# Listing the picked experts by products of one-hots, with prefix products at later ticks and six dense blocks

## The chip, the cores and the metric

The kernel runs on one core of one Trainium2 chip, in one launch. The metric is the device time of an execution in microseconds; less is better. The engines are TensorE (PE, with its weight loads as PEld), VectorE (DVE), ScalarE (ACT), GpSimd (POOL) and SyncE (SP), which only issues transfers here.

## The reference

Two transformer blocks are computed in float32, on 256 tokens of width 2048. The change touches only the last part of the second block, a mixture of 16384 small experts, of which each token picks 16 in each of 8 heads:

```python
def block(xt):
    q = (xt @ wq).reshape(-1, PEER_HEADS, 2, PEER_HALF)
    s = jnp.einsum('thpc,hpnc->thpn', q, keys)
    sv, si = lax.top_k(s, PEER_TOPK)
    ...
    top_s, top_j = lax.top_k(cand, PEER_TOPK)
    eid = jnp.take_along_axis(cid, top_j, axis=-1)
    gate = jax.nn.softmax(top_s.astype(jnp.float32), axis=-1)
    ue = jnp.take(u, eid, axis=0)
    act = jax.nn.gelu(jnp.einsum('thkd,td->thk', ue, xt).astype(jnp.float32), approximate=False)
    ve = jnp.take(v, eid, axis=0)
    return jnp.einsum('thk,thkd->td', (gate * act).astype(xt.dtype), ve)
```

`u` and `v` have 16384 rows of 2048. The result is added to the block's input and normalised.

## The kernel before

Everything ahead of the experts (both blocks' projections, attention, recurrence, the scores and the top-16) is the same in both kernels. What follows has two stages.

**The u loop.** All 16384 experts are multiplied with all tokens: 128 tiles of 128 experts (`i1`), each 128 x 2048 of `u`, loaded in two halves of 512 KB (L94, issued by SP, three buffers). Each half is split into a high and a low float32r part: `whi` is a cast on ACT (L127), `wlo` a subtraction on DVE (L110). From tile 44 on, 16 pairs of matmuls per tile follow (L281 with 512 columns, L282 with 256), then the addition of two halves (L288, L289) and the evacuation (`evac_u`: gelu on ACT, L1383, and a product with the token weights on DVE, L1384). The result of a tile, 128 experts x 256 tokens, stays in SBUF.

Between the matmuls a generator is advanced by `fill.tick()`: after half and at the end of each half tile, so four times per tile once all tokens are weighed. Each tick runs the generator to its next `yield`; what it issues stands at that place in the engines' queues. From tile 44 on it is `weigh`, which makes the weight of every expert for every token out of one-hots (compares on DVE L1240 and on POOL L1242, products on TensorE L1254 and L1257), four tokens at a time. Then `lists` runs.

**`lists`** counts which experts were picked, by which quarters of the tokens (64 tokens each, a code of four bits), and gives each picked expert a place in a list. There are ten classes of codes with 11 or 7 columns of 128 places each (`CLASSES`), and 22 columns (`CA`) for all experts that find no place in their class. Places come from scans along a partition (L1296, L1316) and two products with a triangular matrix over the partitions (the prefix products, L1302 and L1320). Then the number of each picked expert is written to its place in DRAM (`lst`): one indirect write on POOL for each of the 120 tiles (L1340), 128 elements of 4 bytes each; unpicked experts have an address out of bounds. The list is read back (L1348) and turned into two tables of row numbers (L1351 to L1357): `lv` for rows of `v`, `lact` for rows of `rows`.

Meanwhile `keep` copies the finished tiles 0 to 119 to `rows` in DRAM, four tiles (512 KB) at a time, issued by SP between the loads of `u` (L1367): one or two after each tile, as far as tiles are done.

**The v stage.** The output is a sum over blocks of 128 experts: first the dense ones, the tiles from `NKEY` = 120 on, whose rows of `v` are loaded as they stand (L1478); then the blocks of the list, whose rows of `v` and `rows` are gathered by indirect reads on POOL (L1469), into eight slots. Dense and catch-all blocks are split into high and low parts (L1489, L1490 for `v`, L1493, L1494 for the activations) and take 24 matmuls of 512 columns (L1507). A slot's next gather waits for the split or the products that read it. `rest()` handles list columns beyond `CA`; it is skipped at run time unless more than `CA` x 128 experts need the catch-all places. The output's second half is normalised and written at the end.

Of the kernel before, what the change touches and what calls it, by code (L numbers as in the profile page):

```python
# [9 lines left out]
F32 = mybir.dt.float32  # L10
# [3 lines left out]
U32 = mybir.dt.uint32  # L14
I32 = mybir.dt.int32
AF = mybir.ActivationFunctionType
OP = mybir.AluOpType
# [4 lines left out]
D = 2048  # L22
# [19 lines left out]
N1 = 100  # L42
NKEY, CA = 120, 22
CLASSES = {1: 11, 2: 11, 4: 11, 8: 11, 3: 7, 12: 7, 5: 7, 10: 7, 9: 7, 6: 7}
BASE = {c: NKEY + sum(list(CLASSES.values())[:i]) for i, c in enumerate(CLASSES)}
WL = NKEY + sum(CLASSES.values())
BIG = 2.0 ** 20
HELD, SLOTS, LAST = 2, 8, 4
# [143 lines left out]
def block(ctx, tc, a):  # L192
# [58 lines left out]
    def lane(l):  # L251
        return lnp.tile([128, 512], F32, name=f"lane{l}", bufs=2)
# [953 lines left out]
    lst = dp.tile([128 * WL, 1], F32, name="lst")  # L1206
    lst2 = lst.rearrange("(p w) o -> p (w o)", p=128)
    work = pg.tile([128, 2304], F16, name="work")
    el = work.bitcast(F32)[:, 0:WL]
    pool.memset(el, 0.0)  # L1210
    pool.dma_start(lst2, el)
    pool.dma_start(rows[0:1, 0:WL], el[0:1])
# [65 lines left out]
    def lists(l, cnt):  # L1278
# [20 lines left out]
        dve.tensor_copy(tot, w[:, :, NKEY - 1])  # L1299
        yield  # L1300
        ps = lane(l)
# [15 lines left out]
        dve.tensor_copy(ends[:, 0:1], g[:, NKEY - 1:NKEY])  # L1317
        yield
        ps = lane(l)
# [10 lines left out]
        dve.scalar_tensor_tensor(at, place, -1.0, x, op0=OP.add, op1=OP.add)  # L1330
        yield
        dve.tensor_scalar(to, at, 7, None, op0=OP.logical_shift_right)
        dve.tensor_scalar(at, at, 127, None, op0=OP.bitwise_and)
        dve.tensor_copy(x, at)
        dve.scalar_tensor_tensor(at, x, float(WL), to, op0=OP.mult, op1=OP.add)
        e = work.bitcast(F32)[:, 0:NKEY]
        pool.iota(e, pattern=[[128, NKEY]], base=1, channel_multiplier=1, allow_small_or_imprecise_dtypes=True)
        yield
        for i in range(NKEY):
            d = pool.indirect_dma_start(  # L1340
                out=lst, out_offset=bass.IndirectOffsetOnAxis(ap=at[:, i:i + 1], axis=0), in_=e[:, i:i + 1],
                in_offset=None, bounds_check=128 * WL - 1, oob_is_err=False)
            if i:
                tc.declare_no_dep(d.ins, group="scatter", reason="no two experts have one place")
            tc.add_to_no_dep_group("scatter", d.ins)
            if i % 8 == 7:
                yield
        pool.dma_start(el, lst2)  # L1348
        lact, lv = (pg.tile([128, WL], U32, name=n) for n in ("tab", "tab2"))
        places.extend([lact, lv])  # L1350
        pool.tensor_copy(lact, el)  # L1351
        for q in range(4):

            i = BASE[1 << q]
            x = slice(i, i + CLASSES[1 << q])
            pool.tensor_scalar(lact[:, x], el[:, x], 4.0, float(q), op0=OP.mult, op1=OP.add)
        pool.tensor_scalar(lv, el, 1.0, -1.0, op0=OP.max, op1=OP.add)  # L1357
        yield
# [4 lines left out]
    def keep(i, n):  # L1363

        x, j = act_at(i)
        out = rows[1 + i * 128:1 + (i + n) * 128, :].rearrange("(n p) t -> p n t", p=128)
        nc.sync.dma_start(out, x[:, j:j + n, :])  # L1367

    def act_at(i1):
        for i, j, x in acts:  # L1370
            if i1 < j:
                return x, i1 - i
# [162 lines left out]
    def rest():  # L1535

        raw, x = lt[:, 2 * D:3 * D], lt[:, 3 * D:3 * D + T]
        hi = [sp.tile([128, 1024], F32R, name="whi", bufs=BUFS[1]) for _ in range(4)]
        hi, lo = hi[:2], hi[2:]
# [204 lines left out]
```

## Time and profile before

| | |
|---|---|
| median of 3 runs | 2685.31 us (2666.25 to 2693.32) |
| profiled execution: time, span | 2674.23 us, 2672.4 us |
| mean granted clock of TensorE | 0.979 |
| busy: PE, DVE, ACT, POOL | 2530.4, 1598.2, 1027.4, 816.0 us |
| DMA over the span | 535.39 MB, mean 200 GB/s |

The span runs from the first to the last instruction of the profiled execution. The time of a stage is read from its own stretch, not from the totals: the u loop with `weigh` ends its token products at about 1968 us, `lists` follows, the loop's last matmul starts at 2256.3 us, and the v stage's first at 2260.5 us.

### The profile page before, as it was taken

How to read it: one execution, taken by the hardware profiler on the slowest of the kernel's cores; microseconds unless marked ns; L12 is line 12 of the kernel's file. 1: busy time of each engine (PE TensorE's matmuls, PEld its weight loads, DVE VectorE, ACT ScalarE, POOL GpSimd, SP SyncE). 2: the span in 40 equal slices, each digit the busy share in tenths (PEclk: the TensorE clock that was granted, in tenths of full speed). 3: DMA queues.
4: the chain of work that ended last, by engine and by line, in shares of the span. 5: the costliest groups of instructions: out<-in, count | busy, mean ns of one | idle time of the engine just before them, and what ended most of it. 6: DMA issues, size and time to landing. Idle time of an engine off the chain costs nothing. (4 is left out here: it accounts for less than half of the span.)

```text
span 2672.4 us, 39702 instructions
## 1 busy us (share of the span) xinstructions
PE 2530.4 (95%) x14942; PEld 2049.0 (77%) x14942; DVE 1598.2 (60%) x3174; ACT 1027.4 (38%) x1680; POOL 816.0 (31%) x765
## 2 busy tenths in 40 slices
PE   6899999999998999999999999999988779999996
PEld 1588888888877888888899999888876467655553
DVE  3366566544565766666579898899993245322225
ACT  3233334333445444443544445544442234322221
POOL 2000000000012000000201024988937760567763
PEclk8999999999999999999999999999998889999998
DMA  9733334543464555555555555445456457799995
GB/s 363 296 121 124 125 131 162 183 144 119 142 236 162 170 171 167 187 183 189 204 199 184 172 190 173 159 159 165 159 175 183 149 180 291 284 351 367 357 340 198
DMA packets 148808, 535.39 MB, mean 200 GB/s; under 512 B 20392, under 2 KB 35912, under 8 KB 133504
## 3 DMA queue, kind: packets, MB, share of 16 engines
q1 hardware_dynamic: 116352, 378.99, 42.1%
q0 software_dynamic: 32112, 153.51, 15.6%
q8 instruction: 120, 1.97, 0.3%
q14 instruction: 80, 0.66, 0.1%
q10 hardware_dynamic: 144, 0.26, 0.0%
HBM read 512.60 MB, written 20.09 MB: 199 GB/s over the span
## 5 line engine op out<-in xcount | busy, mean ns | idle before, releaser
L110 DVE TENSOR_TENSOR wlo<-raw,whi 128x1024 fp32r<-128x1024 f32 x577 | 703.6, 1223 | 522.3 <-remote 108.7
L127 ACT CAST whi<-raw 128x1024 fp32r<-128x1024 f32 x577 | 605.4, 1052 | 879.5 <-PE acc L281 163.6
L281 PE MATMUL acc<-ga,whi 128*128 128x512 f32 (+1 forms) x2320 | 848.3, 406 | 24.2 <-issue 22.4
L282 PE MATMUL acc<-ga,wlo 128*128 128x256 f32 (+1 forms) x2320 | 661.3, 285 | 23.7 <-issue 20.9
L281 PEld LDWEIGHTS acc<-ga,whi 128*128 128x128 f32 (+1 forms) x2320 | 444.8, 192 | 129.8 <-issue 27.0
L282 PEld LDWEIGHTS acc<-ga,wlo 128*128 128x128 f32 (+1 forms) x2320 | 446.9, 193 | 44.0 <-issue 37.3
L1242 POOL TENSOR_SCALAR work<-iota,tab 128x128 bf16<-128x128 bf16 x256 | 302.0, 1192 | 88.3 <-PE lane L1257 86.1
L276 PE MATMUL acc<-ga,wlo 128*128 128x256 f32 x704 | 199.4, 283 | 1.3 <-DVE wlo L110 1.3
L274 PE MATMUL acc<-ga,whi 128*128 128x256 f32 x704 | 199.5, 283 | 0.0
L275 PE MATMUL acc<-ga,whi 128*128 128x256 f32 x704 | 199.2, 283 | 0.0
L281 PE MATMUL acc<-X,whi 128*128 128x512 f32 x480 | 173.7, 402 | 0.0
L1490 DVE TENSOR_TENSOR act<-fx,act 128x1024 fp32r<-128x1024 f32 x54 | 64.5, 1223 | 163.7 <-ACT act L1489 156.3
L439 POOL DMA_DIRECT2D gw<-in_w_mod x32 | 17.4, 544 | 465.1 <-DVE gate_b L444 333.5
L1340 POOL DMA_INDIRECT lst<-work,tab x120 | 136.2, 1135 | 57.6 <-issue 36.2
L1507 PE MATMUL acc<-act 128*128 128x512 f32 (+1 forms) x500 | 150.3, 417 | 0.0
L1507 PE MATMUL lane<-act 128*128 128x512 f32 (+1 forms) x476 | 141.6, 412 | 3.8 <-ACT act L1493 3.5
L294 PE MATMUL acc<-whi,X 128*128 128x256 f32 x480 | 136.6, 285 | 0.0
L276 PEld LDWEIGHTS acc<-ga,wlo 128*128 128x128 f32 x704 | 135.1, 192 | 1.7 <-DVE wlo L110 1.7
L1469 POOL DMA_INDIRECT act<-rows,tab x108 | 126.3, 1169 | 32.9 <-issue 30.5
L274 PEld LDWEIGHTS acc<-ga,whi 128*128 128x128 f32 x704 | 135.1, 192 | 0.0
L275 PEld LDWEIGHTS acc<-ga,whi 128*128 128x128 f32 x704 | 135.1, 192 | 0.0
L296 PE MATMUL acc<-whi,X 128*128 128x256 f32 x480 | 134.8, 281 | 0.0
(423 smaller groups left out, 4621.7 us busy)
## 6 DMA issues: line engine op xcount, KB each, us to landing
raw<-in_u SPq DMA_DIRECT2D x256, 512.0 KB
raw<-in_w_in SPq DMA_DIRECT2D x240, 512.0 KB
raw<-in_w_mod SPq DMA_DIRECT2D x64, 512.0 KB
raw<-in_w_out SPq DMA_DIRECT2D x64, 512.0 KB
gw<-in_w_mod POOLq DMA_DIRECT2D x32, 512.0 KB
raw<-in_wq SPq DMA_DIRECT2D x32, 512.0 KB
rows<-act SPq DMA_DIRECT2D x17, 512.0 KB
bc<-in_rows POOLq DMA_DIRECT2D x20, 256.0 KB
```

The costliest lines, as they stand in the source:

```text
L110: e.tensor_tensor(lo, raw, hi.bitcast(F32), op=OP.subtract)
L127: nc.scalar.copy(hi, self.raw[c])
L274: mm(ps, w, xh, start=first and own, stop=False, **kw)
L275: mm(ps, w, xl, start=False, stop=False, **kw)
L276: mm(ps, wl, xh, start=False, stop=last, **kw)
L281: mm(ps.rearrange("p (x t) -> p x t", x=2), w, x, start=first, stop=last, skip_group_check=True)
L282: mm(ps[:, :T], wl, x[:, 0], start=False, stop=last, skip_group_check=True)
L294: mm(ps, xh, w, start=first and own, stop=False, **kw)
L296: mm(ps, xl, w, start=False, stop=last, **kw)
L1242: pool.tensor_scalar(o2[:, i], iota2, tab2[:, 0, t:t + 1], tab2[:, 1, t:t + 1], op0=OP.is_equal, op1=OP.mult)
L1340: d = pool.indirect_dma_start(out=lst, out_offset=bass.IndirectOffsetOnAxis(ap=at[:, i:i + 1], axis=0), in_=e[:, i:i + 1], in_offset=None, ...
L1507: mm(out, x, w, start=not (tt, b) in opened, stop=last, skip_group_check=True)
```

## The change

The indirect writes leave `lists`. In their place stand, for each of the now 122 tiles (a column `i` of the tables of places), three compares that make one-hots, and one matmul: the one-hot of the place's partition (128 wide) is the stationary operand, the one-hots of the place's column (108 columns are listed), once times the expert's partition plus one and once times `i`, the moving one; the sum over all columns is the list. POOL makes one of the three in four of five columns. The table is then built on ACT and DVE. The matmul of a column stands three columns later than its compares, in one of five buffers. The prefix products are issued two and three ticks later. Two more tiles are picked from the list rather than taken as dense blocks. The addresses go to DRAM (`atd`) for `rest()`, which now holds the indirect writes and is still skipped unless the catch-all places overflow.

```diff
-NKEY, CA = 120, 22
+NKEY, CA = 122, 22
 ...
+NL = CA + WL - NKEY
 ...
-    pool.dma_start(lst2, el)
 ...
         dve.tensor_copy(tot, w[:, :, NKEY - 1])
-        yield
+
+        for _ in range(3):
+            yield
         ps = lane(l)
         mm(ps[:, 0:n], tri[:, 0], tot, start=True, stop=True)
 ...
         dve.tensor_copy(ends[:, 0:1], g[:, NKEY - 1:NKEY])
-        yield
+        for _ in range(4):
+            yield
         ps = lane(l)
         mm(ps[:, 0:1], tri[:, 0], ends[:, 0:1], start=True, stop=True)
 ...
+        wcols, made = work[:, 0:NL], []
+        bb = work[:, NL + 5 * (128 + 2 * NL):][:, 0:2 * NKEY].bitcast(F32)
+        one = small[:, 40:41]
+        pool.iota(wcols[:, 0:CA], pattern=[[1, CA]], base=0, channel_multiplier=0, allow_small_or_imprecise_dtypes=True)
+        pool.iota(wcols[:, CA:], pattern=[[1, NL - CA]], base=NKEY, channel_multiplier=0,
+                  allow_small_or_imprecise_dtypes=True)
+        pool.iota(one, pattern=[[0, 1]], base=1, channel_multiplier=1, allow_small_or_imprecise_dtypes=True)
         dve.tensor_scalar(to, at, 7, None, op0=OP.logical_shift_right)
+        dve.tensor_copy(bb, to)
         dve.tensor_scalar(at, at, 127, None, op0=OP.bitwise_and)
         dve.tensor_copy(x, at)
         dve.scalar_tensor_tensor(at, x, float(WL), to, op0=OP.mult, op1=OP.add)
-        e = work.bitcast(F32)[:, 0:NKEY]
-        pool.iota(e, pattern=[[128, NKEY]], base=1, channel_multiplier=1, allow_small_or_imprecise_dtypes=True)
-        yield
-        for i in range(NKEY):
-            d = pool.indirect_dma_start(
-                out=lst, out_offset=bass.IndirectOffsetOnAxis(ap=at[:, i:i + 1], axis=0), in_=e[:, i:i + 1],
-                in_offset=None, bounds_check=128 * WL - 1, oob_is_err=False)
 ...
-            if i % 8 == 7:
-                yield
-        pool.dma_start(el, lst2)
+        pool.dma_start(atd, at)
+        yield
+
+
+        ps = lane(l)
+
+        def put(i):
+            y = work[:, NL + i % 5 * (128 + 2 * NL):][:, 0:128 + 2 * NL]
+            dve.tensor_scalar(y[:, 0:128], iota, x[:, i:i + 1], None, op0=OP.is_equal)
+            e = dve if i % 5 == 4 else pool
+            e.tensor_scalar(y[:, 128:128 + NL], wcols, bb[:, i:i + 1], one, op0=OP.is_equal, op1=OP.mult)
+            dve.tensor_scalar(y[:, 128 + NL:], wcols, bb[:, i:i + 1], float(i), op0=OP.is_equal, op1=OP.mult)
+            return y
+
+        for i in range(NKEY + 3):
+            if i < NKEY:
+                made.append(put(i))
+            if i >= 3:
+                y = made.pop(0)
+                mm(ps[:, 0:2 * NL], y[:, 0:128], y[:, 128:], start=i == 3, stop=i == NKEY + 2)
+            if i % 4 != 3:
+                yield
+        yield
+        f = work.bitcast(F32)[:, 0:2 * NL].rearrange("p (j n) -> p j n", j=2)
+        act.copy(f[:, 0], ps[:, 0:NL])
+        dve.scalar_tensor_tensor(f[:, 1], ps[:, NL:2 * NL], 128.0, f[:, 0], op0=OP.mult, op1=OP.add)
         lact, lv = (pg.tile([128, WL], U32, name=n) for n in ("tab", "tab2"))
         places.extend([lact, lv])
-        pool.tensor_copy(lact, el)
+        for k, n, m in ((0, 0, CA), (CA, NKEY, NL - CA)):
+            y = f[:, 1, k:k + m]
+            dve.tensor_scalar(lv[:, n:n + m], y, 1.0, -1.0, op0=OP.max, op1=OP.add)
+            dve.tensor_copy(lact[:, n:n + m], y)
 ...
     def keep(i, n):
 
+        n = min(n, NKEY - i)
 ...
     def rest():
 
         raw, x = lt[:, 2 * D:3 * D], lt[:, 3 * D:3 * D + T]
+        at = lt[:, 3 * D + T:][:, 0:NKEY].bitcast(U32)
+        e = lt[:, 3 * D + T + 128:][:, 0:NKEY]
+        el = lt[:, 3 * D + 2 * T:][:, 0:WL]
+        pool.memset(el, 0.0)
+        pool.dma_start(lst2, el)
+        pool.dma_start(at, atd)
 ...
```

The lines of the changed kernel are numbered by its own file, so L110, L281 and L1469 of before are L111, L282 and L1499 there.

On POOL's queue, from the last one-hots of `weigh` (L1242) to the first gathers of the v stage (L1469), before:

```order
L1242 TENSOR_SCALAR work<-iota_11885,tab_11884 128x128 x256
L1337 IOTA work 128x120
L1340 DMA lst<-work,tab 26368x1 x120
L1348 DMA work<-lst 128x206
L1351 CAST tab<-work 128x206
L1356 TENSOR_SCALAR tab<-work 128x11 x4
L1357 TENSOR_SCALAR tab_20547<-work 128x206
L1469 DMA fx<-in_v,tab_20547 128x2048
L1469 DMA act_21790<-rows,tab 128x256
```

The same stretch of POOL's queue in the changed kernel (L1243 are the one-hots of `weigh`, L1359 the compares of the list, L1499 the gathers):

```order
L1243 TENSOR_SCALAR work<-iota_11885,tab_11884 128x128 x256
L1340 IOTA work 128x22
L1341 IOTA work 128x86
L1343 IOTA small 128x1
L1349 DMA atd<-tab 128x122
L1359 TENSOR_SCALAR work<-work,small 128x108 x98
L1499 DMA late<-in_v,tab_21757 128x2048
L1499 DMA act_21929<-rows,tab 128x256
L1499 DMA late<-in_v,tab_21757 128x2048
L1499 DMA act_21929<-rows,tab 128x256
```

The 120 indirect writes, the readback and the conversions behind them are gone; 98 compares stand there, and the first two gathers now go to the slots in `late`, which the two dense blocks had.

On DVE's queue, from the last step of the place table (L1335) on, before (L110 is the split, L1384 and L289 the loop's evacuation):

```order
L1335 SCALAR_TENSOR_TENSOR tab<-tab 128x120
L110 TENSOR_TENSOR wlo<-raw,whi 128x1024
L1384 SCALAR_TENSOR_TENSOR act_15086<-act_15086,acc 128x256
L110 TENSOR_TENSOR wlo<-raw,whi 128x1024
L289 TENSOR_TENSOR acc<-acc,half 128x256
L110 TENSOR_TENSOR wlo<-raw,whi 128x1024
L1384 SCALAR_TENSOR_TENSOR act_15086<-act_15086,acc 128x256
L110 TENSOR_TENSOR wlo<-raw,whi 128x1024
L289 TENSOR_TENSOR acc<-acc,half 128x256
```

The same place in the changed kernel (L1348 is the last step of the place table, L111 the split, L1414 and L290 the evacuation, L1357 to L1360 the compares of the list):

```order
L1348 SCALAR_TENSOR_TENSOR tab<-tab 128x122
L111 TENSOR_TENSOR wlo<-raw,whi 128x1024
L1414 SCALAR_TENSOR_TENSOR act_15086<-act_15086,acc 128x256
L1357 TENSOR_SCALAR work<-iota,tab 128x128
L1360 TENSOR_SCALAR work<-work 128x108
L1357 TENSOR_SCALAR work<-iota,tab 128x128
L1360 TENSOR_SCALAR work<-work 128x108
L111 TENSOR_TENSOR wlo<-raw,whi 128x1024
L290 TENSOR_TENSOR acc<-acc,half 128x256
L1357 TENSOR_SCALAR work<-iota,tab 128x128
L1360 TENSOR_SCALAR work<-work 128x108
L1357 TENSOR_SCALAR work<-iota,tab 128x128
```

Between the splits of the loop, which stood alone with its evacuation steps, now stand the compares of two or three list columns at a time.

On TensorE's queue, one half tile in the same part of the changed kernel (L1368 are the list's products, L282 and L283 the loop's):

```order
L1368 LDWEIGHTS work
L1368 MATMUL lane_20060<-work 128x216
L282 MATMUL acc<-ga,whi 128x512
L283 MATMUL acc<-ga,wlo 128x256
L282 MATMUL acc<-ga,whi 128x512
L283 MATMUL acc<-ga,wlo 128x256
L282 MATMUL acc<-ga,whi 128x512
L283 MATMUL acc<-ga,wlo 128x256
L282 MATMUL acc<-ga,whi 128x512
L283 MATMUL acc<-ga,wlo 128x256
L1368 LDWEIGHTS work
L1368 MATMUL lane_20060<-work 128x216
```

Before, only the loop's matmuls stood here; now one or two products of the list come after every fourth pair.

## Rows read from the trace of the kernel before

**Rows 1.** The page's slices: busy tenths of TensorE in 40 equal parts.

```profile
PE   6899999999998999999999999999988779999996
```

**Rows 2.** Stretches: length; busy PE, PEld, DVE, ACT, POOL; clock; DMA share; GB/s.

```profile
1640.00:1975.00 335.00, 332.86 (x2393) 289.37 (x2392) 303.20 (x945) 164.51 (x398) 294.72 (x250) 1.00 0.49 161
1975.00:2011.00 36.00, 27.39 (x128) 23.43 (x127) 32.26 (x95) 9.87 (x16) 0.23 (x1) 0.81 0.62 198
2011.00:2020.00 9.00, 9.00 (x54) 7.93 (x54) 4.96 (x6) 3.98 (x6) 6.73 (x7) 1.00 0.86 252
2028.00:2176.00 148.00, 104.80 (x387) 73.46 (x387) 39.88 (x49) 32.71 (x50) 116.93 (x103) 0.86 0.50 150
2190.00:2245.00 55.00, 55.00 (x313) 47.67 (x312) 32.65 (x41) 27.48 (x42) 3.09 (x6) 1.00 0.69 224
...
2310.00:2630.00 320.00, 319.96 (x1410) 171.44 (x1409) 87.82 (x98) 75.57 (x99) 217.45 (x197) 1.00 0.92 349
```

**Rows 3.** L281 by stretch: length; busy PE, PEld; clock; DMA share; GB/s.

```profile
1640.00:1975.00 335.00, 292.46 (x819) 153.46 (x818) 1.00 0.49 161
1975.00:2020.00 45.00, 34.69 (x87) 18.51 (x86) 0.85 0.67 209
2028.00:2176.00 148.00, 88.00 (x193) 43.44 (x194) 0.86 0.50 150
2190.00:2245.00 55.00, 55.00 (x157) 29.20 (x156) 1.00 0.69 224
1975.00:2257.00 282.00, 208.61 (x518) 107.34 (x517) 0.90 0.59 189
```

**Rows 4.** TensorE's waits, 1975 to 2190 us: total, times, longest.

```profile
PE acc L281 <- issue: 22.4, 45, 1.2
PE acc L282 <- issue: 20.9, 42, 1.0
PE lane L1302 <- issue: 4.5, 1, 4.5
PE lane L1320 <- DVE small L1317: 4.1, 1, 4.1
```

**Rows 5.** Timeline of TensorE: start us, length us, instruction, idle before it.

```profile
2049.14 0.28 PE L282 MATMUL acc<-ga,wlo 128*128 128x256 f32 x1 [0.93 <-issue]
...
2050.59 0.39 PE L281 MATMUL acc<-ga,whi 128*128 128x512 f32 x1 [0.47 <-issue]
```

**Rows 6.** Timeline of POOL in the same stretch.

```profile
2048.66 0.97 POOL L1340 DMA_INDIRECT lst<-work,tab  x1 [0.30 <-issue]
2049.93 0.97 POOL L1340 DMA_INDIRECT lst<-work,tab  x1 [0.30 <-issue]
```

**Rows 7.** Line of the indirect writes: ns min/median/max, first and last start.

```profile
L1340 POOL DMA_INDIRECT lst<-work,tab x120: 967/971/1857, 2011.4 to 2183.0; - x120
```

**Rows 8.** Timeline of DVE while tokens are weighed, columns as in rows 5.

```profile
1704.34 0.43 DVE L289 TENSOR_TENSOR acc<-acc,half 128x256 f32<-128x256 f32 x1 [0.67 <-ACT half L288]
1704.68 1.87 DVE L1240 TENSOR_SCALAR work<-iota,tab 128x128 f16<-128x128 f16 x8
1706.46 1.22 DVE L110 TENSOR_TENSOR wlo<-raw,whi 128x1024 fp32r<-128x1024 f32 x1
1707.60 0.20 DVE L1384 SCALAR_TENSOR_TENSOR act<-act,acc 128x48 f32<-128x48 f32 x1
```

**Rows 9.** Groups of instructions, 1640 to 1975 us: busy us, mean ns; idle before.

```profile
L1242 POOL TENSOR_SCALAR work<-iota,tab 128x128 bf16<-128x128 bf16 x250 | 295.2, 1193 | 88.3 <-PE lane L1257 86.1 <-PE lane L1254 2.2
```

**Rows 10.** Timeline of POOL in the v stage: two gathers behind dense blocks.

```profile
2277.21 1.00 POOL L1469 DMA_INDIRECT fx<-in_v,tab  x1 [2.12 <-DVE act L1490]
...
2282.66 1.00 POOL L1469 DMA_INDIRECT act<-in_v,tab  x1 [2.12 <-DVE act L1490]
```

**Rows 11.** The line of the rows writes, columns as in rows 7.

```profile
L1367 SPq DMA_DIRECT2D rows<-fx x8: 427/428/500, 1976.0 to 2019.1; - x8
L1367 SPq DMA_DIRECT2D rows<-late x5: 429/436/1392, 2164.9 to 2221.9; - x5
```

More of the change, by code (lines that the diff above doesn't have):

```diff
@@ L1207, in block @@
     lst2 = lst.rearrange("(p w) o -> p (w o)", p=128)
+    atd = dp.tile([128, NKEY], U32, name="atd")
     work = pg.tile([128, 2304], F16, name="work")
@@ L1335, in lists @@
         dve.scalar_tensor_tensor(at, x, float(WL), to, op0=OP.mult, op1=OP.add)
-        e = work.bitcast(F32)[:, 0:NKEY]
-        pool.iota(e, pattern=[[128, NKEY]], base=1, channel_multiplier=1, allow_small_or_imprecise_dtypes=True)
+        pool.dma_start(atd, at)
         yield
-        for i in range(NKEY):
-            d = pool.indirect_dma_start(
-                out=lst, out_offset=bass.IndirectOffsetOnAxis(ap=at[:, i:i + 1], axis=0), in_=e[:, i:i + 1],
-                in_offset=None, bounds_check=128 * WL - 1, oob_is_err=False)
-            if i:
-                tc.declare_no_dep(d.ins, group="scatter", reason="no two experts have one place")
-            tc.add_to_no_dep_group("scatter", d.ins)
-            if i % 8 == 7:
+        ps = lane(l)
@@ L1352, in lists @@
         for q in range(4):
             i = BASE[1 << q]
-            x = slice(i, i + CLASSES[1 << q])
-            pool.tensor_scalar(lact[:, x], el[:, x], 4.0, float(q), op0=OP.mult, op1=OP.add)
-        pool.tensor_scalar(lv, el, 1.0, -1.0, op0=OP.max, op1=OP.add)
+            n = CLASSES[1 << q]
+            dve.tensor_scalar(lact[:, i:i + n], f[:, 1, i - NKEY + CA:i - NKEY + CA + n], 4.0, float(q), op0=OP.mult,
+                              op1=OP.add)
         yield
@@ L1537, in rest @@
         raw, x = lt[:, 2 * D:3 * D], lt[:, 3 * D:3 * D + T]
+        at = lt[:, 3 * D + T:][:, 0:NKEY].bitcast(U32)
[4 more added lines that the diff above has]
+        pool.dma_start(at, atd)
+        pool.iota(e, pattern=[[128, NKEY]], base=1, channel_multiplier=1, allow_small_or_imprecise_dtypes=True)
+        for i in range(NKEY):
+            d = pool.indirect_dma_start(
+                out=lst, out_offset=bass.IndirectOffsetOnAxis(ap=at[:, i:i + 1], axis=0), in_=e[:, i:i + 1],
+                in_offset=None, bounds_check=128 * WL - 1, oob_is_err=False)
+            if i:
+                tc.declare_no_dep(d.ins, group="scatter", reason="no two experts have one place")
+            tc.add_to_no_dep_group("scatter", d.ins)
+        pool.dma_start(el, lst2)
+        pool.tensor_copy(lact[:, CA:NKEY], el[:, CA:NKEY])
+        pool.tensor_scalar(lv[:, CA:NKEY], el[:, CA:NKEY], 1.0, -1.0, op0=OP.max, op1=OP.add)
         hi = [sp.tile([128, 1024], F32R, name="whi", bufs=BUFS[1]) for _ in range(4)]
```

## Prediction

> **What bounds the kernel now.** I read the page's slices first, then the busy table of single stretches, the waits of TensorE, its timeline, and last the rows of the engines that take new work. The slices [rows 1] are to show one thing: TensorE is at 9 tenths nearly everywhere from the fifth slice on, and the one long dip (8, 7, 7, 9) lies at about 2000 to 2270 us. That is the end of the u loop, while POOL writes the list of picked experts.
>
> The stretches say what a tile of the u loop costs. A tile has 16 matmuls of L281. In 2190 to 2245 us, with nothing beside the loop, 157 of them take 55 us: 5.61 us per tile. In 1640 to 1975 us, where the one-hots of the 256 tokens ride along, 819 take 335 us: 6.54 us. In 2028 to 2176 us, 193 take 148 us: 12.27 us [rows 3]. From 1975 to 2257 us there are 518, or 32.4 tiles; at 5.61 us these are 181.5 us, so **100.5 us of the 282 are lost there**, and that is what the change can reach before the tail.
>
> What takes them? TensorE waits 4.5 us and 4.1 us once each, for the two prefix products (L1302, L1320), and some 43 us in 87 short pieces put down to "issue", that is, to nothing that the profile shows [rows 4]. Two of the pieces end at 2049.14 and 2050.59 us, 0.48 and 0.66 us after an indirect write starts on POOL at 2048.66 and 2049.93 us [rows 5, 6]. The 120 writes run from 2011.4 to 2183.0 us [rows 7]. The rows writes (`keep`) started earlier, at 1976.0 us, and one still comes at 2221.9 us [rows 11]; with them alone, and the first seven indirect writes, TensorE was busy 9.00 of 9 us at full clock (2011 to 2020 us), and it is busy 55 of 55 after the last indirect write [rows 2]. So I put the stall down to the indirect writes. The rest of the loss is the granted clock of 0.86 in 2028 to 2176 us and of 0.81 around the two waits [rows 2], and tiles that start late behind these.
>
> The tail is bound by TensorE: 1410 matmuls in 320 us, never waiting (319.96 us busy), with DMA at 0.92 [rows 2]. That is 0.227 us per matmul. A dense block has 3 terms, 2 token halves and 4 banks, 24 matmuls, hence 5.45 us; the gathers that follow each dense block's split are indeed 5.45 us apart [rows 10].
>
> **The change, part by part.**
>
> *Indirect writes gone.* The 120 writes, the readback (L1348) and POOL's five conversions leave the path. With them go the 43 us of short waits and the clock that they cost.
>
> *List by products.* 122 columns; each costs TensorE one matmul of 216 columns, DVE two compares (a third in every fifth), POOL one compare in four of five.
> TensorE: in 1640 to 1975 us 2393 matmuls ran, 1638 of them the loop's; the other 755, of 128 columns, made a tile 0.94 us longer, 14.8 per tile, so 0.064 us each. Scaled by 216/128 that is 0.107 us, times 122 = **13 us** (not below 7.7, the unscaled price; not above 27.7, the 0.227 us of a tail matmul with 512 columns).
> DVE: eight one-hot compares of 128 columns with two per-partition scalars start 1.78 us before the next instruction, 0.22 us each; a split takes 1.14 us until the next starts, the addition of the halves 0.34 [rows 8], and I take as much for the last step (L1384), which has the same shape. A tile of the loop is thus 2.95 us of DVE. The code ticks four times per tile and yields three times in four columns, so a tile carries 5.33 columns: 2.2 x 0.22 x 5.33 = 2.6 us (the new compares have fewer columns or scalars, so this is an upper estimate). 5.6 us of DVE beside 5.61 + 5.33 x 0.107 = 6.18 us of TensorE: it fits, as it did in 1640 to 1975 us, where DVE was busy 90% and TensorE 99% [rows 2].
> POOL: 1.19 us per compare there [rows 9]; 4.27 per tile are 5.1 us of 6.18. It fits. Its only other work, one write of the addresses (`atd`), is issued before the first column. The matmul of a column stands three columns behind its compares, so a late compare has some 3.5 us before TensorE waits.
>
> *Prefix products later.* Two and three more ticks (1.4 us each) are put ahead of the two products. But DVE was busy 32.26 of the 36 us there [rows 2]: the 128 matmuls in them are 4 tiles, 11.8 us of its loop work, and 20.5 us are the list's scans. Spread over 20 ticks, five tiles, DVE needs 20.5 + 14.7 = 35.2 us where TensorE needs 28.0. The wait moves from the products to the splits (wlo, L110), behind which the loop's next matmuls queue. I take **7 us**; at best 0 (the lag is swallowed by the two chunks that are split ahead), at worst what this part costs today, 45 us for 87 matmuls of L281 [rows 3] less 5.44 x 5.61 = 14.5 us.
>
> *Transfers.* Faster tiles bring the rows writes closer together: 1.5 per tile of 0.52 MB beside 1.05 MB of u, 1.83 MB in 6.18 us, or 297 GB/s for some 18 tiles. Before, the most beside rows writes was 252 GB/s at a DMA share of 0.86 [rows 2]. If 252 GB/s is a ceiling, a tile takes 7.28 us, 20 us over 18 tiles; if a share of 1 can be reached (293 GB/s), 2 us. SP issues both, in order, so a u load stands behind up to two rows writes. I take **7 us**, nearer the lower end, since at 0.86 TensorE did not wait at all.
>
> *122 instead of 120 tiles picked; dense blocks six instead of eight.* One more rows write, of half size, four tiles before the end of the loop. Computed from the reference's inputs, 2696 experts fall to the 2816 catch-all places (2653 of them before), so `rest` stays skipped, and all that was added to it. Two dense blocks fewer are 2 x 5.45 = **10.9 us** off the tail. The cover they gave: the gathers had 8 dense blocks ahead, now 6 (33 us). But two gathers need no slot to come free and start when the list is done: its last matmul stands four tiles (22 us) before the loop's end. Bound below: 5 us, if the DMA share of 0.92 lets only half through.
>
> *Sum.* The stretch of 282 us becomes 181.5 + 13 + 7 + 7 = 208.5, 73.5 less; with the tail 84.4. The profiled execution took 2674.2 us, so **2590 us**. The median of the runs shown, 2685.3, lies 11 us above that execution; the range's upper part allows for it.
>
> The Trainium skill ("SBUF — State Buffer", section "SBUF: two separate sides") says that on the engine side only the port pair shared by VectorE and GpSimd is contended, and that PE never waits on anyone. By that page an indirect write on POOL could not hold up TensorE through SBUF, and the pieces would have another cause; the sum would then be that of the first rival, 2669 us. No row here shows the way by which a write stops TensorE, only that pieces and writes go together, and the sum follows the rows.
>
> **The rivals.**
>
> *The rows writes, not the indirect ones, cause the stall.* For it: both run through the whole slow stretch. Against: 9.00 of 9 us busy with rows writes dense. Then only the prefix waits (14.5 - 7) and the tail (10.9) are gained, less 13: 2669 us.
>
> *The transfers pace the stage.* At 209 GB/s, the mean of the 45 us from 1975 on [rows 3], taken as a ceiling, a tile takes 8.8 us, 47 us more over 18 tiles instead of 7: 2630 us.
>
> *Everything hides.* No head wait, no transfer cost, 7.7 us of matmuls: 181.5 + 7.7, and 2674.2 - 92.8 - 10.9 = 2570 us.
>
> *DVE and POOL take turns (slower).* If a compare on one blocks the other for its whole length, a column needs 0.8 x 1.19 + 2.2 x 0.22 + 2.95/5.33 = 2.0 us in turn instead of 1.16, and TensorE waits for each column's product in its queue: 122 x 0.83 = 102 us more, 2692 us, slower. It decides from 1.16 + 84.4/122 = 1.85 us per column. Against it: in 335 us DVE was busy 303.20 and POOL 294.72 [rows 2], which taking turns would not allow. The Trainium skill, in the same page and section, calls the shared pair an exclusive lock held for a whole instruction; the trace does not agree for these compares, and 2692 us is what that rule would give.
>
> **How the numbers follow.** The forecast (2575 to 2605 us) 0.62; transfers (2605 to 2640) 0.15; everything hides (2565 to 2575) 0.12; rows writes 0.06; taking turns 0.05. A change within 1% is about what a measurement cannot tell from none; that is 2647 to 2701 us. The first three cases lie below it, and a part of the last two: faster 0.90, same 0.07, slower 0.03. Eight in ten: 2568 to 2622 us.
>
> **What would show it.** Right, if tiles from 1975 us take 6 to 6.5 us with a granted clock near 1, TensorE's "issue" pieces are gone, the u loop ends near 2183 us, and six dense blocks end some 33 us after it. The transfer case shows as casts waiting for raw<-in_u; taking turns as matmuls of L1368 waiting for POOL, with compares over 1.5 us; the head as wlo splits late between 1975 and 2010 us. The forecast is wrong if pieces of "issue" stay though no indirect write runs.

## The result, and the profile after

The changed kernel took 2594.69 us (median of 6 runs, 2592.27 to 2600.92), the kernel before, run beside it, 2680.8 us (6 runs, 2666.25 to 2702.9): **ratio 0.9676, 95% interval 0.9628 to 0.9724**, faster. The profiled execution, the longest of the six, took 2600.92 us, its span is 2599.0 us. Ratios here and below leave out runs more than 1.5% above the fastest of the same kernel: none here, three of the seven of the kernel before on the third chip. In the changed kernel L128 is the whi cast and L1537 a matmul of the v stage.

The page's slices of the changed kernel, to be held against [rows 1]: the dip at 2000 to 2270 us is gone, and the granted clock stays at 9 tenths or more there, slice by slice.

```profile
PE   5899999999998999999999999999999999999996
PEclk8999999999999999999999999999999999999998
```

The busy table of its stretches (us, then busy time and count of each engine, granted clock, DMA share, GB/s), to be held against [rows 2]. They are the loop with the tokens' one-hots, the head (scans and prefix products), the list's columns with one or two rows writes to a tile beside them, the columns with a rows write to every fourth tile only, the end of the loop, and the tail.

```profile
1640.00:1979.00 339.00, 336.64 (x2416) 291.95 (x2415) 306.24 (x956) 165.59 (x398) 295.42 (x250) 1.00 0.49 160
1979.00:2029.00 50.00, 41.88 (x210) 34.73 (x209) 41.49 (x117) 16.34 (x26) 7.46 (x10) 0.91 0.68 214
2029.00:2109.00 80.00, 75.99 (x450) 61.23 (x449) 60.91 (x189) 31.56 (x48) 54.83 (x53) 0.99 0.82 278
2109.00:2170.00 61.00, 61.00 (x367) 49.70 (x366) 52.23 (x157) 26.34 (x40) 47.37 (x41) 1.00 0.62 208
2170.00:2194.00 24.00, 24.00 (x141) 20.93 (x140) 12.06 (x25) 7.89 (x15) 5.21 (x4) 1.00 0.86 335
2200.00:2560.00 360.00, 360.00 (x1579) 204.69 (x1578) 106.85 (x120) 89.91 (x117) 234.43 (x212) 0.99 0.91 347
```

From the evacuation of the tile with which the token weights end (at 1975.6 us before, 1979.4 us after, read from DVE's timeline) to the start of the loop's last matmul (2256.7 us before, 2194.0 us after), which I call the stage, it is 281.1 us before and **214.6 us** after: 66.5 us less. From the first v matmul to the end, the tail, it is 411.9 and **401.2 us**: 10.7 less. The 3.8 us by which the stage begins later lie ahead of the change. Two matmuls mark the border in the changed kernel's TensorE timeline (start, duration):

```profile
2194.00 0.28 PE L283 MATMUL acc<-ga,wlo 128*128 128x256 f32 x1
2197.81 1.22 PE L1537 MATMUL lane<-act 128*128 128x512 f32 x2 [3.53 <-ACT act L1523]
```

What TensorE waits for in the stage (us in total, times, longest), where [rows 4] had over 40 us put down to "issue":

```profile
PE lane L1368 <- DVE work L1360: 4.6, 5, 1.5
PE acc L283 <- DVE wlo L111: 3.2, 2, 3.0
PE lane L1368 <- DVE work L1357: 1.6, 1, 1.6
PE lane L1305 <- DVE small L1300: 1.6, 1, 1.6
PE lane L1324 <- DVE small L1320: 1.0, 1, 1.0
```

And what the list's columns cost in 2025 to 2170 us (count, busy us, mean ns, idle before):

```profile
L1359 POOL TENSOR_SCALAR work<-work,small 128x108 f16<-128x108 f16 x97 | 107.8, 1118 | 37.2 <-PE lane L1368 36.8
...
L1357 DVE TENSOR_SCALAR work<-iota,tab 128x128 f16<-128x128 f16 x120 | 31.7, 264 | 0.0
L1360 DVE TENSOR_SCALAR work<-work 128x108 f16<-128x108 f16 x120 | 30.2, 252 | 0.0
L1368 PE MATMUL lane<-work 128*128 128x216 f16 x118 | 26.9, 266 | 5.6 <-DVE work L1360 4.0 <-DVE work L1357 1.6
```

The tiles between the evacuations at 2108.9 and 2170.2 us took 6.13 us each (10 tiles, with a rows write to every fourth), those from 2036.3 to 2108.9 us 6.60 us (11 tiles, with one or two rows writes each), and the first six of the stage, the head, 49.6 us, where six clean ones are 33.7.

### The profile page after: what moved, and what is told of

It reads as the page before. It is cut to its first block, busy times and chain, and to the rows that moved or that the text cites. A ratio compares the mean times of both kernels' runs of the same rounds, so it can differ in the third digit from the quotient of the medians.

```text
span 2599.0 us, 39956 instructions
## 1 busy us (share of the span) xinstructions
PE 2497.0 (96%) x15016; PEld 2029.2 (78%) x15016; DVE 1637.3 (63%) x3446; ACT 1021.3 (39%) x1675; POOL 781.1 (30%) x738
## 5 line engine op out<-in xcount | busy, mean ns | idle before, releaser
L111 DVE TENSOR_TENSOR wlo<-raw,whi 128x1024 fp32r<-128x1024 f32 x577 | 703.1, 1223 | 396.0 <-issue 91.9
L128 ACT CAST whi<-raw 128x1024 fp32r<-128x1024 f32 x577 | 605.2, 1052 | 821.4 <-PE acc L282 175.7
L282 PE MATMUL acc<-ga,whi 128*128 128x512 f32 (+1 forms) x2320 | 839.0, 403 | 0.0
L283 PE MATMUL acc<-ga,wlo 128*128 128x256 f32 (+1 forms) x2320 | 651.8, 281 | 6.7 <-DVE wlo L111 6.5
L282 PEld LDWEIGHTS acc<-ga,whi 128*128 128x128 f32 (+1 forms) x2320 | 437.7, 189 | 97.9 <-issue 1.8
L283 PEld LDWEIGHTS acc<-ga,wlo 128*128 128x128 f32 (+1 forms) x2320 | 439.5, 189 | 10.2 <-DVE wlo L111 10.2
L1243 POOL TENSOR_SCALAR work<-iota,tab 128x128 bf16<-128x128 bf16 x256 | 302.2, 1191 | 89.2 <-PE lane L1258 89.2
L276 PE MATMUL acc<-ga,whi 128*128 128x256 f32 x704 | 199.9, 284 | 0.0
L282 PE MATMUL acc<-X,whi 128*128 128x512 f32 x480 | 173.7, 402 | 0.0
L1537 PE MATMUL lane<-act 128*128 128x512 f32 (+1 forms) x484 | 148.4, 426 | 3.8 <-ACT act L1523 3.5
L1520 DVE TENSOR_TENSOR act<-fx,act 128x1024 fp32r<-128x1024 f32 x44 | 52.9, 1228 | 147.4 <-ACT act L1519 111.9
L1537 PE MATMUL acc<-act 128*128 128x512 f32 (+1 forms) x468 | 140.8, 420 | 0.0
L290 DVE TENSOR_TENSOR acc<-acc,half 128x256 f32<-128x256 f32 x175 | 75.3, 430 | 102.0 <-ACT half L289 96.7
L1499 POOL DMA_INDIRECT act<-rows,tab x108 | 124.2, 1150 | 41.3 <-issue 29.9
```

The costliest lines, as they stand in the source:

```text
L111: e.tensor_tensor(lo, raw, hi.bitcast(F32), op=OP.subtract)
L128: nc.scalar.copy(hi, self.raw[c])
L276: mm(ps, w, xl, start=False, stop=False, **kw)
L282: mm(ps.rearrange("p (x t) -> p x t", x=2), w, x, start=first, stop=last, skip_group_check=True)
L283: mm(ps[:, :T], wl, x[:, 0], start=False, stop=last, skip_group_check=True)
L1243: pool.tensor_scalar(o2[:, i], iota2, tab2[:, 0, t:t + 1], tab2[:, 1, t:t + 1], op0=OP.is_equal, op1=OP.mult)
```

## The experiments

They ran on three chips; each section says which. Which chip the result's own runs had is not known. The kernel before took 2705.16 us on the first (1 run), 2674.22 to 2736.39 us on the third (7 runs), but **2591.67 and 2592.09 to 2596.75 us on the second** (1 run and 9). That decides how the kernels with indirect writes are to be read, and was itself the largest surprise. In each kernel I count TensorE's matmuls in stretches of 17.4 us, about twelve back-to-back writes: about 100 when nothing holds the loop up. In the profiled execution of the kernel before it is 39 to 49 from 2031 to 2152 us.

### Indirect writes without rows writes, and with nothing written (first chip)

The theory was that the indirect writes stall TensorE; the rivals were the rows writes and the traffic. Both are edits of the kernel before.

```diff
-        if done["tokens"] == T:
-            for _ in range(1 + i1 % 2):
+        if done["tokens"] == T and i1 >= 116:
+            for _ in range(3):
```

> The kernel before, with its rows writes put off to the last dozen u tiles, so that the 120 indirect writes run with no rows write beside them. If the indirect writes themselves stall TensorE (the theory of the prediction): between the first and the last indirect write the tiles still take 11 to 12 us each, the 90 or so short pieces in which TensorE waits for nothing shown are still there, 35 to 45 us of them, and the u loop ends no more than 10 us earlier than the 2256 us of before. If the rows writes cause the stall, or the two together by their traffic: tiles of 5.6 to 6.5 us, the pieces gone, the u loop ending about 80 us earlier.

```diff
-        dve.scalar_tensor_tensor(at, x, float(WL), to, op0=OP.mult, op1=OP.add)
+        dve.scalar_tensor_tensor(at, x, float(WL << 9), to, op0=OP.mult, op1=OP.add)
```

> The kernel before, with every place of the list multiplied so far that it lies out of bounds, but for the places on row 0: the 120 indirect writes are still issued by POOL, with the same 120 x 1.15 us or so, but almost nothing is written (so the list is nearly empty and the later gathers all take row 0: this part of the computation is left out). If what stalls TensorE is the written packets: the short pieces are gone and the tiles take 5.6 to 6.6 us, the u loop ends about 75 us before 2256. If it is the issuing on POOL (the descriptors being made and put into the queue): tiles of 11 to 12 us as before, u loop end within 10 us of 2256.

Measured: 2697.89 and 2690.21 us, stages of 296.9 and 292.1 us. The busy table of the kernel without rows writes:

```profile
2014.00:2031.00 17.00, 17.00 (x98) 14.76 (x97) 8.12 (x11) 6.39 (x11) 13.40 (x12) 1.00 0.59 168
2031.00:2048.40 17.40, 13.55 (x59) 10.19 (x58) 4.92 (x7) 3.92 (x7) 13.76 (x12) 0.90 0.31 92
2048.40:2065.80 17.40, 12.68 (x51) 9.04 (x51) 4.87 (x7) 4.08 (x7) 13.75 (x12) 0.90 0.31 91
...
2152.40:2168.00 15.60, 8.86 (x29) 5.72 (x27) 1.56 (x2) 1.46 (x3) 11.88 (x13) 0.67 0.18 55
```

and of the kernel that writes next to nothing:

```profile
2031.00:2048.40 17.40, 12.22 (x45) 8.19 (x45) 4.95 (x6) 3.96 (x6) 13.74 (x13) 0.90 0.42 117
2048.40:2065.80 17.40, 12.95 (x48) 9.59 (x48) 4.87 (x6) 4.06 (x6) 13.75 (x13) 0.80 0.54 164
```

The first dozen writes leave TensorE alone (98 matmuls in 17 us). Then its rate halves, at 92 GB/s as at 164, with the data landing or not. Beside the last two dozen writes it falls further, at a granted clock of 0.67 and less. The profiled execution of the kernel before does not do so (43 and 49 matmuls in the same stretches), and so these stages are longer than its 281.1 us; why is open. The loops end at 2275.2 and 2270.5 us; the second text had its end within 10 us of 2256. There is no trace of the kernel before from this chip; it took longer there (2705.16 us) than both edits. TensorE's waits from 2031 to 2153 us, without rows writes and then with nothing written, are of the old kind:

```profile
PE acc L282 <- issue: 14.1, 33, 0.9
PE acc L281 <- issue: 10.7, 26, 1.0
```

```profile
PE acc L282 <- issue: 18.0, 43, 0.9
PE acc L281 <- issue: 13.6, 29, 1.1
```

So neither the rows writes nor what lands in the list causes the stall. That leaves POOL's issuing, but also the packets of the writes' own queue, which the second edit does not remove: the profile has 764 of them from 2031 to 2064 us, and 768 in the kernel before. The pieces go with the single writes: in the kernel before, 78 of 89 pieces between 2026 and 2184 us end 0.4 to 1.1 us after a write starts, where a write starts every 1.44 us, so that chance would put about half there.

### Half of the writes, and plain writes (second chip)

```diff
         for i in range(NKEY):
-            d = pool.indirect_dma_start(
...
+            if i % 2 == 0:
+                d = pool.indirect_dma_start(
```

> The kernel before with only every second indirect write (60 of 120, four instead of eight to a tile; the list is half empty, so half of the picked experts are left out of the gathers). The two kernels e3 and e4 showed that TensorE crawls beside the indirect writes with no rows write near and with nothing written, about 45 to 48 matmuls in the 17.4 us of twelve writes where 96 ran beside the first twelve. If each write issued on POOL costs TensorE its own share: the loss over the stage halves, tiles beside the writes of 8.5 to 9.5 us, u loop ends 30 to 45 us earlier than the 2256 us of before. If it is a matter of the stage as such (tiles are paced by something else, whatever POOL does): 11 to 12 us per tile still, or, if four writes fit in a tile without harm, 5.6 to 6.6 us.

```diff
-            d = pool.indirect_dma_start(
...
+            pool.dma_start(lst2[:, i:i + 1], e[:, i:i + 1])
```

> The kernel before with each indirect write replaced by a plain transfer of the same 128 x 4 bytes, issued by POOL too, to column i of the list (the list then holds every row in order instead of the picked ones: that part of the result is left out). If any transfer that POOL issues in small pieces stalls TensorE: pieces of 0.3 to 1 us again, tiles of over 8 us. If it takes the indirect form, with POOL working out the addresses: no pieces, tiles of 5.6 to 6.6 us, u loop ends near 2180 us, as in the changed kernel or before it.

Measured: 2596.26 and 2605.67 us, with the kernel before at 2591.67. Neither could tell the theories apart, because nothing stalls on this chip. In the first, POOL still issued its 60 writes back to back (one per 1.40 us on average), since no engine paces it, and TensorE kept its full rate:

```profile
2031.00:2048.40 17.40, 17.40 (x103) 15.22 (x102) 9.25 (x12) 8.53 (x13) 13.74 (x13) 1.00 0.84 276
```

POOL does here what it did on the first chip (13.74 us busy with 13 writes), and 276 GB/s go beside it. The plain writes made the stage 212.1 us against 199.3. TensorE waited 10.1 us for splits there (6.1 for wlo, 4.0 for whi) against 4.0 us, and no piece is put down to nothing but the wait for the first prefix product. The whi casts waited 56.8 us for u loads from 2011 to 2120 us, but 52.9 us beside the half of the writes too, so their total does not explain the difference; that its pieces are longer (up to 5.6 us against 4.2) may.

### Three kinds of writes in one run (third chip), and spaced writes first (second chip)

To be free of the chip, one kernel holds three parts: 40 writes as before, 40 plain ones, and 40 indirect ones with a compare on POOL between.

```diff
+            if 40 <= i < 80:
+                pool.dma_start(lst2[:, i:i + 1], e[:, i:i + 1])
+            else:
...
+                if i >= 80:
+                    pool.tensor_scalar(work[:, 1024:1152].bitcast(BF16), iota2, e[:, i:i + 1], e[:, i:i + 1],
+                                       op0=OP.is_equal, op1=OP.mult)
```

> The kernel before with its 120 indirect writes in three parts: 40 as they were, back to back; then 40 plain transfers of the same size to columns of the list; then 40 indirect writes with a compare of 128 x 128 on POOL between them, so that they come half as often (the list holds wrong rows in places, so the result of the last stage is not the reference's). On a chip where the kernel before takes about 2680 us, if the indirect form stalls TensorE: about 45 matmuls in the 17.4 us of twelve writes in the first part, 90 or more per 17 us in the plain part, and in the third part a loss per write that is the same (0.9 us or so each, 8.5 to 9.5 us a tile) or, if it takes a dense row of writes, none. If any small transfer of POOL does it, the second part crawls too. On a chip where the kernel before takes about 2590 us (one such was seen: 2591.7 us): no crawl in any part, tiles of 5.6 to 7 us throughout, which is then the trace of indirect writes that do not stall.

Measured: 2619.11 us, with the kernel before at 2711.33 us (median of 7). The busy table: one stretch for the first dozen writes, two for the rest of the dense part, two for the plain part, two for the spaced part.

```profile
2011.00:2028.00 17.00, 16.56 (x96) 14.37 (x95) 6.52 (x8) 5.30 (x8) 12.99 (x13) 1.00 0.84 250
2028.00:2045.40 17.40, 12.25 (x43) 8.09 (x42) 4.86 (x6) 4.06 (x6) 13.79 (x12) 0.86 0.39 111
2045.40:2062.80 17.40, 12.28 (x47) 9.09 (x46) 4.87 (x6) 3.96 (x6) 13.86 (x12) 0.85 0.56 164
2073.00:2090.40 17.40, 16.17 (x93) 13.88 (x92) 7.78 (x10) 5.49 (x9) 8.96 (x17) 1.00 0.89 250
2090.40:2113.00 22.60, 19.45 (x93) 16.12 (x92) 9.97 (x14) 9.03 (x14) 11.95 (x23) 0.85 0.81 238
...
2147.80:2165.20 17.40, 17.40 (x102) 15.35 (x101) 10.86 (x15) 9.38 (x15) 16.05 (x13) 1.00 0.77 234
2165.20:2182.60 17.40, 17.40 (x103) 15.35 (x102) 10.68 (x13) 8.29 (x13) 15.99 (x14) 1.00 0.74 227
```

In one run the same instruction takes half of TensorE's rate in a dense row (43 and 47 matmuls) and none of it when a compare stands between, so that one comes every 2.7 us instead of every 1.4 (102 and 103). The second half of the plain part is slower as well (93 matmuls in 22.6 us), but not by pieces put down to nothing. All that TensorE waits for from 2072 to 2113 us, the plain part, and then from 2113 to 2182 us, the spaced part, is splits:

```profile
PE acc L282 <- DVE wlo L110: 3.2, 3, 1.4
PE acc L281 <- ACT whi L127: 1.2, 1, 1.2
```

```profile
PE acc L282 <- DVE wlo L110: 0.7, 1, 0.7
```

The plain transfers leave the same packets on the writes' queue as the indirect ones, and 40 of them came in some 40 us, so packets of this kind alone are not the cause either. Two things are not told apart: the spacing, and the compare that makes it.

A piece of the dense part, TensorE and then POOL (start, duration, in brackets the idle time before): POOL's write of 2036.28 us lasts 1.76 us. TensorE, slower at first (0.57 us for a matmul that takes 0.39 later; granted clock 0.69 from 2032 to 2036 us), stands still from 2037.97 on and goes on 0.50 us after the next write starts.

```profile
2036.58 0.57 PE L281 MATMUL acc<-ga,whi 128*128 128x512 f32 x1
...
2037.69 0.28 PE L282 MATMUL acc<-ga,wlo 128*128 128x256 f32 x1
2038.84 0.39 PE L281 MATMUL acc<-ga,whi 128*128 128x512 f32 x1 [0.86 <-issue]
```

```profile
2036.28 1.76 POOL L1343 DMA_INDIRECT lst<-work,tab  x1 [0.30 <-issue]
2038.34 0.97 POOL L1343 DMA_INDIRECT lst<-work,tab  x1 [0.30 <-issue]
```

The spaced part came last, behind plain transfers. A kernel with 40 spaced writes first and 50 dense ones behind was to tell whether the place mattered.

```diff
-        for i in range(NKEY):
+        for i in range(90):
...
+            if i < 40:
+                pool.tensor_scalar(work[:, 1024:1152].bitcast(BF16), iota2, e[:, i:i + 1], e[:, i:i + 1],
+                                       op0=OP.is_equal, op1=OP.mult)
```

> The kernel before with 90 of its 120 indirect writes (the other columns are left out of the list, so of the result of the last stage too): 40 with a compare of 128 x 128 on POOL behind each, so that one comes every 2.7 us, and then 50 back to back. In the kernel with three parts the spaced writes came last and did not stall TensorE. If spacing is what frees it: 90 to 100 matmuls in 17.4 us beside the first 40, then, after about twelve of the dense ones, 40 to 50 in 17.4 us, in the same run. If it was the place (the end of the row, or something that the plain transfers ahead had set right): the crawl comes beside the spaced writes too, or in neither part. On a chip where the kernel before takes about 2592 us: no crawl in either part, which is then the trace of dense writes that do not stall.

It met the second chip: 2592.38 us (8 runs), kernel before 2594.88 us (9 runs), ratio 0.9992 (0.9981 to 1.0004). On the place it says nothing; it gives the trace of dense writes that do not stall, here its last two stretches of them:

```profile
2135.40:2152.80 17.40, 17.40 (x100) 15.09 (x99) 10.16 (x13) 8.12 (x13) 13.74 (x13) 1.00 0.70 220
2152.80:2170.20 17.40, 17.40 (x100) 15.05 (x99) 10.25 (x13) 7.03 (x12) 13.73 (x13) 1.00 0.74 267
```

Its stage is 199.9 us long, its tail 412.9 us.

### The changed kernel again (third chip)

> The changed kernel itself, unaltered, timed again beside the kernel before on this chip. If the saving of the u loop is the stall that the indirect writes cause, and the chip decides whether they do: where the kernel before takes 2665 to 2705 us, the changed one takes 2590 to 2600, ratio 0.962 to 0.973; where the kernel before takes about 2592 us, the changed one gains only the two dense blocks (10.9 us) and loses the products, their compares and the head, 13 to 20 us: 2588 to 2602 us, ratio 0.998 to 1.004. If the saving had another cause: 0.967 whatever the chip.

2594.72 us (4 runs, 2591.08 to 2599.48), ratio 0.9628 (0.9515 to 0.9741) to a kernel before that spread over 62 us, too widely to call the ratio clear; stage 213.5, tail 399.8 us. The changed kernel itself ran only where the kernel before takes over 2660 us. For the second chip there is an estimate: a stage 14 us longer than the 199.9 there, a tail 12 us shorter (next experiment); that is no difference.

### Eight dense blocks, and the prefix products put back (first chip)

```diff
-NKEY, CA = 122, 22
+NKEY, CA = 120, 22
```

> The changed kernel with eight dense blocks again (two fewer columns in the list). Theory of the prediction: the tail from the first v matmul to the end is 2 x 5.45 = 10.9 us longer than the 401.2 us of the changed kernel, 412 us; the u loop ends where it did or 0.2 us earlier. Rival: a block fewer is a pair of gathers that come late anyway, and the tail changes by less than 5 us.

```diff
-        for _ in range(3):
-            yield
+        yield
...
-        for _ in range(4):
-            yield
+        yield
```

> The changed kernel with the two prefix products put back to one tile after their scans, as in the kernel before. If the later products are worth what their waits were before (4.5 + 4.1 us): the waits of TensorE for the two results come back, and the seven tiles after the start of the list work take 55 to 58 us instead of 49.6. If the head is bound by VectorE, which is late with the wlo splits whatever TensorE waits for: the same 16 us are lost, under other names, and the u loop ends within 2 us of the changed kernel's 2194.

2612.89 and 2598.35 us. The tails are 415.5 and 404.1 us on the same chip: two dense blocks are 11.4 us, if the ticks, in which the two also differ, do not touch the tail. The stages are 213.0 and 212.0 us: the earlier products cost nothing. The waits for them are back, the wait for wlo is gone, and the first six tiles (they are what the 49.6 us above are of) take 49.9 us, against 49.0 in the kernel with eight blocks on the same chip:

```profile
PE lane L1303 <- issue: 4.6, 1, 4.6
PE lane L1321 <- DVE small L1318: 4.5, 1, 4.5
PE lane L1365 <- DVE work L1357: 2.0, 4, 0.9
```

### Even rows writes, spread scans, and all of it with four dense blocks

On the second chip, edits of the changed kernel:

```diff
-            for _ in range(1 + i1 % 2):
+            for _ in range(1):
```

> The changed kernel with one rows write to a tile instead of one or two in turn. The prediction gave the transfers 7 us; the changed kernel's tiles took 6.6 us beside rows writes and 6.13 us without. If that difference is the traffic peak of u loads and rows writes together: tiles beside rows writes of 6.2 to 6.3 us, over more tiles, and the u loop ends 2 to 5 us earlier than 2194 us. If it is the bytes as such, whenever they come: the loop ends within 1.5 us of 2194.

```diff
-            if i % 3 == 2:
-                yield
+            yield
...
-            if i % 2:
-                yield
+            yield
...
-            if i % 4 != 3:
+            if i % 3 != 2:
```

> The changed kernel with the scans and the placement of the ten classes cut into one class to a tile (instead of three, and two), the prefix products one tile after them again, and three columns of the list in two tiles instead of four in three, so that the whole still ends within the u loop. If the 16 us lost at the head come from VectorE's bursts (three scans of a class take 6 to 7 us beside a tile of 5.6): the loss there falls to 4 to 8 us, and the u loop ends 5 to 10 us earlier than 2194 us, unless the denser columns (1.5 products to a tile, 6.2 to 6.4 us a tile) give some of it back. If the head's loss is the prefix products' waits or the rows writes: 14 to 18 us still.

2587.72 us, stage 207.8 us, 6.17 us per tile (21 tiles with a rows write each, 2030.3 to 2159.9 us); and 2583.43 us, stage 204.4 us, the first nine tiles 60.2 us instead of 70.4. (The "tile" that one class takes, by the text on the second kernel, is a tick, a quarter of a tile.) Both went the way that was expected, and further: the loops end 10.5 and 14.5 us before 2194 us, the stages are 6.8 and 10.2 us shorter than the changed kernel's 214.6, where 2 to 5 and 5 to 10 us were expected. Neither has a changed kernel beside it on that chip, so the third chip had both edits, the later products and four dense blocks together:

```diff
-NKEY, CA = 122, 22
+NKEY, CA = 124, 22
```

> The changed kernel with one rows write to a tile, the scans and the placement one class to a tile step, three columns in two steps, and 124 instead of 122 columns, so that four dense blocks are left instead of six. From the two earlier kernels: the spread head is worth 6 to 10 us and the even rows writes 3 to 6 us of the u loop, not quite in sum, since both fill the same tiles; the two dense blocks 2 x 5.45 = 10.9 us of the tail. Expected 15 to 25 us below the changed kernel on the same chip, 2570 to 2580 us. If the gathers that follow the list are now late for lack of cover (four blocks of 5.45 us in place of six): a wait of TensorE in the first steps of the v stage and only 5 to 12 us in all.

**2571.65 us** (4 runs, 2571.29 to 2573.14), ratio 0.9542 (0.9433 to 0.9651) to the kernel before (with the same spread of that one), and 23.1 us below the changed kernel's 2594.72 on the same chip, whose runs do not overlap with it. Stage 202.8 instead of 213.5, its first nine tiles 59.8 instead of 68.9, tail 388.2 instead of 399.8 us. What TensorE still waits for between 1975 and 2184 us:

```profile
PE lane L1534 <- ACT act L1520: 3.5, 1, 3.5
PE lane L1365 <- DVE work L1357: 2.8, 1, 2.8
PE acc L283 <- DVE wlo L111: 1.8, 4, 0.7
```

## Why the prediction was right, and where it was not

*The indirect writes stall TensorE*: right, on two of the three chips. The prediction inferred it from pieces and writes that go together [rows 4 to 7]; the runs without rows writes, with next to nothing written and with three kinds of writes show it. One of its arguments was no evidence: the 9.00 of 9 us busy beside rows writes [rows 2] held seven indirect writes as well, and the first dozen of these stall nothing. The rivals of the rows writes (2669 us) and of the transfers as the stage's pace (2630 us) fall: the stall stays without the former, and the changed kernel carried 278 GB/s at 6.6 us a tile. What the prediction took for a property of the kernel belongs to kernel and chip together: on the second chip, both times it was met, the stall is not there, and the change would gain nothing that is clear of noise by the estimate above. Whether it is the chip itself or something else that went with it no run tells.

*List products, 13 us*: 6.13 instead of 5.61 us per tile with 5.33 columns is 0.098 us each (0.107 forecast), 12 us. *Transfers, 7 us*: 0.47 us over 11 tiles, 5 us; the nearer end was the right choice. The casts wait 25.3 us for u loads there, and what reaches TensorE are late compares (L1360, 4.0 us); with one rows write to a tile the 6.60 us become 6.17. *DVE and POOL taking turns (2692 us)*: DVE was busy 52.23 and POOL 47.37 of 61 us, so these compares did not. *Everything hides (2570 us)*: not so; the products alone cost 12 us.

*Tail, 10.9 us*: 10.7 between the two profiled executions, 11.4 and 11.6 in the pairs on one chip.

*The head, 7 us*: **the term that was mis-sized**. It measured 16 us (49.6 less 33.7). The prediction saw rightly that DVE's scans are the work there and that the wait would move from the products to wlo [rows 2, 4]. Its 7 us are DVE's 35.2 us of work less the 28.0 us of five tiles, as if DVE worked on without a pause once the products stand later. The work was about right (DVE was busy 36.1 us in these five tiles), but they took 43.2 us: between its bursts DVE waited, 4.9 us of it for what ACT makes out of TensorE's sums. The later ticks cure nothing, as the kernel without them shows: DVE has the same bursts between the same tiles, and on the second chip the kernel with 90 indirect writes needs 50.2 us for these six tiles as well. What helps is to cut the bursts: one class to a tick, as the first nine tiles on the second and third chips show. An estimate says why: in DVE's timeline a class's scan takes 0.67 us until the next starts, and with a quarter of the loop's own 2.95 us per tile that is 1.41 us, about one tick (1.40 us); three classes are 2.75 us. The place of a class takes 1.16 us, so one to a tick still overfills it: the head gets shorter, not free.

With the measured terms the stage is 181.5 + 12 + 16 + 5 = 214.5 us, against 214.6. The forecast's 208.5 is 6 us short of it: the head's 9 us less what the other terms gave back. The median lies 4.7 us above 2590, and that closeness is in part luck: the profiled execution before was faster than the median of its runs, the one after the slowest of its six, and the runs of the two kernels spread over 37 and 9 us. A chip of the second kind was in none of the prediction's cases.

TensorE is held up though next to nothing is written, and goes free when a compare stands between the issues; by which way the indirect writes reach it, why the first dozen are free, and why one chip is spared, is open. Whether spaced writes are free wherever they stand in the row is open too, since that kernel met the chip without the stall. The Trainium skill ("SBUF — State Buffer", section "SBUF: two separate sides") says that PE never waits on anyone on the engine side of that memory; no run here shows whether the stall comes through it or by another way, so the runs neither bear this out nor refute it.

## What to carry to other kernels

Pieces of idle time that a profile puts down to nothing, beside another engine's row of issues, can be real and large: test them by moving, emptying and spacing that engine's work before rebuilding the algorithm, since here, in one run, a short POOL instruction between the writes went with no stall too. Run the kernel before on more than one chip before crediting a change with what it removes. When work on a side engine delays a main loop, cut it into pieces that the side engine finishes within one step of the loop; moving only the instruction that waits for it moves the wait.

## What the runs showed of the hardware that was not expected

- The same program took 2591.67 to 2596.75 us on one chip (10 runs) and 2666.25 to 2736.39 us in all other runs. By the traces of the kernels with its dense indirect writes, the difference lies beside these: 39 to 59 matmuls in 17.4 us behind the first dozen writes (fewer at the end of two runs), or 87 to 103.
- Indirect writes whose addresses lie out of bounds slow TensorE as those that land do (45 and 48 matmuls in 17.4 us).
- In one run on a chip that stalls: 43 matmuls in 17.4 us beside a write every 1.4 us, 102 beside one every 2.7 us.
- On the chip without the stall, 120 plain transfers of 128 four-byte pieces cost more than 60 or 90 indirect ones (stage 212.1 against 199.3 and 199.9 us).
